# The squares for the MLP's norm, taken from the copy in DRAM during the first up groups

## The chip, the cores and the metric

One Trainium2 chip; the kernel runs on one of its cores. The metric is the time of one execution in device microseconds (us). The kernel before took 2325.93 us, the median of three runs (2322.78 to 2328.96).

A core has five engines that each work through their own instructions in order and wait for each other by semaphores: TensorE (PE, matrix products into the banks of PSUM), VectorE (DVE), ScalarE (ACT), GpSimd (POOL), and SyncE (SP), which here only issues transfers. SP's transfers go over eight lanes in turn (DMAHW0 to 7 in the orders below), POOL's over lanes named DMASW; a transfer waits for the one before it on its lane.

## The reference

One layer of an encoder block on 512 tokens of width 2048, in float32:

```
h   = rmsnorm(x, g_mix)                        # projection, two mixers side by side
x   = x + concat(mla, dsa) @ w_out             # 2048 x 2048
x   = x + cross_attention(rmsnorm(x, g_cross)) # ends in w_o_cross, 512 x 2048
hm  = rmsnorm(x, g_mlp)
x   = x + square(relu(hm @ w_up)) @ w_down     # 2048 x 8192 and 8192 x 2048
y   = rmsnorm(x, g_final)

rmsnorm(x, g) = x * rsqrt(mean(x * x, -1) + 1e-6) * g
```

The case is about the norm in front of the MLP. The kernel doesn't scale hm before the product: it multiplies the raw x with the gains into w_up and applies the squared factor 1/rms^2 to square(relu(...)) afterwards, so the factor is needed only when the first group of up is finished.

## The kernel before

All activations are kept transposed, features on the 128 partitions and the 512 tokens in the row. x is 16 tiles `res[0]` to `res[15]` of 128x512.

**Up.** 16 groups of 8 units. A unit is a Strassen-like step of 7 products with 6 matmuls of 128x256 each (42 matmuls, L308); the 8 units of a group add into the same 7 of 8 PSUM banks, products in the order p1, q6, p7, q4, p2, q5, p3. A unit needs its weights as a split: `load_blocks` issues three SP transfers into a ring of four buffers (L1461, L1463, L1465), POOL adds a further block by an accumulating transfer (L1470), and the split makes two sums on VectorE and, twice, a cast on ScalarE ("hi") and the rest on VectorE ("lo"), one part of 1024 and one of 768 columns. A ring buffer is free again when the split of the unit four before is done. A unit also needs the pair q of x (q is its number in the group, made once by `gen_xpair(q)`: gains on ScalarE, four sums, casts and lo parts).

**The end of a group** (`gen_up_out`, L1537): the 7 banks are emptied, the first (p1) by a ScalarE copy into e1, a part of the buffer G; then relu and square on ScalarE (four passes of 128x1024), the multiplication with `bc` (the squared 1/rms of each token, spread over the partitions) on VectorE, four sums, and two SP stores of 896 KB from G to `tp_dram` (L1596). G and its companion CT are there once: the next group's e1 goes into the part that these stores read.

**The squares.** `residual1(n)` (L1376) finishes a residual tile after the cross attention: it adds, spawns the pair of every second tile, stores the tile to `xs_dram` (L1385; down reads it again), squares it on ScalarE and adds the square to `acc_r` on POOL (L1393). When all 16 are in, `gen_rstd_l` (L1425) sums over the partitions by four ones-matmuls (L303, bank<-ones), takes the power -1/2 (VectorE, then POOL, `small<-small,nhalf`), spreads it by four transposes (L328) and a ScalarE copy into `bc`, and squares `bc` on VectorE.

The ring of the weights lies where residual tiles lay. So the loads of the first three units wait for the pairs that read those tiles, `("xg", q)`, and for the squares, `("sq", 1, 3)` and `("sq", 1, 7)` (L1449, L1451).

**What sets the order.** The kernel is written as generators that yield until something is ready. A planner (`Plan`, `Planned`) keeps a clock for each engine from fixed costs and lets the generators go on in the order of these clocks, which becomes the order of the instructions on each engine. It knows what TensorE, VectorE, ScalarE and POOL write and read, and of the transfers only what is told to it by `plan.issue("dma", ...)`; of the stores to `tp_dram` it is told nothing. The semaphores are placed afterwards for every true dependence, the reads of stores among them.

Of the kernel before, what the change touches and what calls it, by code (L numbers as in the profile page):

```python
# [11 lines left out]
AF = mybir.ActivationFunctionType  # L12
OP = mybir.AluOpType
# [4 lines left out]
KT = 16  # L18
# [140 lines left out]
def kernel(  # L159
# [20 lines left out]
    nc = tc.nc  # L180
# [3 lines left out]
    plan = Plan()  # L184
    act = Planned(nc.scalar, plan, "act")
    dve = Planned(nc.vector, plan, "dve")
    pool = Planned(nc.gpsimd, plan, "pool")
    rt = plan.ready
# [11 lines left out]
    xs_dram = nc.dram_tensor("xs_dram", (KT, 128, 512), F32, kind="Internal").ap()  # L200
# [12 lines left out]
    def fslot(i, n=512):  # L213
        return fb[:, i : i + n]
# [6 lines left out]
    res = [fslot(4096 + 512 * i) for i in range(8)] + [fslot(512 * i) for i in range(8)]  # L221
# [21 lines left out]
    flag = set()  # L243
# [16 lines left out]
    def step():  # L260
        for t in list(tasks):
            if not t.done and t.at <= plan.clk["pe"]:
                t.go()

    def spawn(gen, first=False):
        t = Task(gen)
        if first:
            tasks.insert(0, t)
        else:
            tasks.append(t)  # L270
        return t

    def until(cond):
        idle = 0
        while not cond():
            n = plan.count
            step()
            if plan.count == n and not cond():
                later = [t.at for t in tasks if t.at > plan.clk["pe"]]
                if later:  # L280
                    plan.clk["pe"] = min(later)
                else:
                    idle += 1
                    assert idle < 200, "schedule is stuck"
            else:
                idle = 0
# [89 lines left out]
    def rstd_tokens(dst, accs, ntb, n, home):  # L376

        yield rt(*accs)
        b = (yield from take(home))[0]
        for tb in range(ntb):  # L380
            for j, a in enumerate(accs):
                mm(b[:, 2 * tb : 2 * tb + 2], a[:, tb * 128 : tb * 128 + 128], ones,
                   j == 0, j == len(accs) - 1)
        yield rt(b)
        rsqrt_mean(dst, b[:, 0 : 2 * ntb : 2], n)
        home.put(b)
# [674 lines left out]
    acc_r, sq_r = s2[2], [s2[0], s2[1]]  # L1061
# [297 lines left out]
    sq_x = s2[4]  # L1359
# [16 lines left out]
    def residual1(n, b):  # L1376

        yield rt(b, res[n])
        dve.tensor_tensor(res[n], res[n], b, op=OP.add)
        banks_f.put(b)  # L1380
        flag.add(("x1", n))
        if n % 2:
            spawn(gen_xpair(n // 2), True)
        yield rt(res[n])
        nc.sync.dma_start(xs_dram[n], res[n])  # L1385
        while n > 0 and ("sq", 1, n - 1) not in flag:
            yield 0
        if n == 0:
            act.activation(acc_r, res[n], AF.Square)
        else:  # L1390
            act.activation(sq_x, res[n], AF.Square)
            yield rt(sq_x)
            pool.tensor_tensor(acc_r, acc_r, sq_x, op=OP.add)  # L1393
        flag.add(("sq", 1, n))

    def sums(dst, b12, b11, b21, b22, eng):
        t1, t2, t3, t4 = dst
# [5 lines left out]
    def gen_xpair(q):  # L1403

        while ("x1", 2 * q) not in flag or ("x1", 2 * q + 1) not in flag:
            yield 0
        gx = (yield from take(gxbufs))[0]
        x1, x2 = res[2 * q], res[2 * q + 1]
        g1, g2 = (g_mlp[:, 2 * q + j : 2 * q + j + 1] for j in range(2))
        yield rt(x1, x2)  # L1410
        act.activation(gx[:, 0:256], x1[:, 256:512], AF.Copy, scale=g1)
        act.activation(gx[:, 512:1024], x2, AF.Copy, scale=g2)
        act.activation(gx[:, 256:512], x1[:, 0:256], AF.Copy, scale=g1)
        yield rt(gx)
        c = lambda i: gx[:, 256 * i : 256 * i + 256]
        flag.add(("xg", q))
        sums([c(4), c(5), c(6), c(7)], c(0), c(1), c(2), c(3), dve)
        pr = yield from take_pair(q)
        for a, n in ((0, 768), (768, 1024)):
            src = gx[:, 256 + a : 256 + a + n]  # L1420
            yield from hi_lo(pr[:, a : a + n], pr[:, 1792 + a : 1792 + a + n], src)
        gxbufs.put(gx)
        XP[q] = pr

    def gen_rstd_l():  # L1425
        while ("sq", 1, 15) not in flag:
            yield 0
        yield from rstd_tokens(rstd_l, [acc_r], 4, D, banks_f)
        yield from spread(bc, rstd_l, 4)
        yield rt(bc)  # L1430
        dve.tensor_tensor(bc, bc, bc, op=OP.mult)
        flag.add("bc")

    def spread(dst, tok, ntb):

        yield rt(tok)
        b = (yield from take(banks_f))[0]
        for tb in range(ntb):
            transpose(blk(b, tb), tok[:, tb : tb + 1].to_broadcast([128, 128]))
        yield rt(b)  # L1440
        act.copy(dst, b[:, 0 : 128 * ntb])
        banks_f.put(b)


    def load_blocks(i):

        k = i - first_s
        if k == 0:
            need = lambda: all(("xg", q) in flag for q in range(2)) and ("sq", 1, 3) in flag  # L1449
        elif k < 3:  # L1450
            need = lambda: all(("xg", q) in flag for q in range(4)) and ("sq", 1, 7) in flag  # L1451
        elif k == 3:
            need = lambda: first_s - 2 in splits and splits[first_s - 2].done
        else:
            need = lambda: i - 4 in splits and splits[i - 4].done
        while not need():
            yield 0
        r, src = ring[k % 4], units[i].src
        s31 = r[:, 768:1280]
        a21 = src[:, 0:256].unsqueeze(1).to_broadcast([128, 2, 256])  # L1460
        nc.sync.dma_start(s31.rearrange("p (u c) -> p u c", u=2), a21)  # L1461
        plan.issue("dma", 800.0, [s31], [], 3800)
        nc.sync.dma_start(r[:, 0:512], src[:, 256:768])  # L1463
        plan.issue("dma", 800.0, [r[:, 0:512]], [], 3800)
        nc.sync.dma_start(r[:, 1536:1792], src[:, 768:1024])  # L1465
        plan.issue("dma", 400.0, [r[:, 1536:1792]], [], 3800)

        def add_blocks():
            yield rt(s31)
            nc.gpsimd.dma_start(s31, src[:, 256:768], accum_op=OP.add)  # L1470
            plan.issue("pool", 1250.0, [s31], [s31], 5000)
            flag.add(("load", i))

        spawn(add_blocks(), True)
# [29 lines left out]
    def strassen_pe(i, st, pair, first, last, order):  # L1504

        hi, lo = HI[units[i].buf], LO[units[i].buf]
        until(lambda: ("sa", i) in flag)
        for x, r in enumerate(order):
            w, t = PRODUCTS[r]
            if x == 4:  # L1510
                flag.add(("pa", i))
                until(lambda: ("sb", i) in flag)
            one_product(st, r, hi, lo, 256 * w, pair, t, first, last)
# [85 lines left out]
    def up_units(g):  # L1599
        st = {}  # L1600

        def pe(kk):
            def run(i):
                if g == 0 and kk == 0:
                    spawn(gen_rstd_l())
                until(lambda: kk in XP)
                if kk == 7:
                    spawn(gen_up_out(g, st), True)
                strassen_pe(i, st, XP[kk], kk == 0, kk == 7, ORDER)
                if g == 15:  # L1610
                    pace(2)
            return run

        return [Unit(w_up[g * 8 + kk], 1024, pe(kk)) for kk in range(8)]
# [11 lines left out]
    def pace(n):  # L1626
        for _ in range(n):
            if paced[0] < 4 * NLOAD:
                spawn(gen_load_t(*divmod(paced[0], 4)))
                paced[0] += 1  # L1630
# [350 lines left out]
    def loader():  # L1981
        for i, u in enumerate(units):
            if i >= first_s:
                yield from load_blocks(i)
                continue
            while i >= 3 and not (i - 3 in splits and splits[i - 3].done):
                yield 0
            more = u.load() if u.load is not None else iter(())
            for t in more:
                if t is True:  # L1990
                    break
                yield t
            if u.src is not None:
                dma(wraw[u.buf][:, 0 : u.n], u.src)
            yield from more
            flag.add(("load", i))
# [145 lines left out]
```

## Time and profile before

| | |
|---|---|
| median of 3 runs | 2325.93 us |
| profiled execution, its own time | 2329.6 us |
| its span (first to last instruction) | 2327.5 us |
| mean granted clock of TensorE | 0.991 of 2.4 GHz |
| TensorE busy | 2251.6 us, 97% |
| VectorE busy | 1662.7 us, 71% |
| ScalarE busy | 1067.2 us, 46% |
| POOL busy | 411.0 us, 18% |

The times of the rows are from the span's start. The residual tiles are made from about 911 to 949 us, up runs from 948 to about 1640. A busy share is a mean over stages; a stage is read from its own stretch. "Idle before" is the time an engine stood still before an instruction, with what released it.

### The profile page before, as it was taken

The numbers are of one execution on the slowest core, as the hardware profiler recorded it, in microseconds if no ns is written. First come the engines' busy times: TensorE is split into PE (matmuls) and PEld (weight loads), VectorE is DVE, ScalarE is ACT, GpSimd is POOL, SyncE is SP. The second block draws the span as 40 slices with busy tenths as digits, with TensorE's granted clock in tenths as the row PEclk, the third lists the DMA queues.
The fourth block names the chain that finished last, engine by engine and source line by source line (L and its number), as shares of the span: only waits on it lengthen the run. The fifth ranks groups of instructions, "written<-read, shape, count | busy, mean of one in ns | idle before, by whom it ended". The sixth has DMA issues, their size and how long they took to land.

```text
span 2327.5 us, 41732 instructions
## 1 busy us (share of the span) xinstructions
PE 2251.6 (97%) x16056; PEld 2165.0 (93%) x16056; DVE 1662.7 (71%) x2629; ACT 1067.2 (46%) x1506; POOL 411.0 (18%) x493
## 2 busy tenths in 40 slices
PE   8999999999999999899999999999999999999996
PEld 8999999998888787799999999999999999999996
DVE  7678543447834547978678787877977877877886
ACT  6542433345523446645354454545444444444453
POOL 3110010103001101411111111111112231111142
PEclk9999999999999999899999999999999999999998
DMA  5322222231243434687888978789889998778863
GB/s 174 103 89 89 68 82 75 71 109 46 82 150 113 144 132 155 169 211 202 226 223 215 251 209 248 205 231 277 245 237 245 231 230 233 219 215 232 220 172 107
DMA packets 272103, 403.56 MB, mean 173 GB/s; under 512 B 23552, under 2 KB 175120, under 8 KB 271648
## 3 DMA queue, kind: packets, MB, share of 16 engines
q1 hardware_dynamic: 229376, 328.41, 43.2%
q0 software_dynamic: 41296, 71.40, 18.2%
q8 instruction: 125, 2.05, 0.4%
q10 hardware_dynamic: 1232, 1.09, 0.2%
q14 instruction: 74, 0.61, 0.1%
HBM read 363.07 MB, written 37.75 MB: 172 GB/s over the span
## 4 chain that ended last, share of the span: by engine, by line
PE 65%; DVE 15%; DMA 11%; issue 5%; POOL 2%; ACT 1%; SPq 1%; DVEq 0%; POOLq 0%; ACTq 0%
PE bank L303 33%; PE bank L308 30%; DMA fb<-in_w_up_dram 7%; DVE fb L139 7%; DVE hl L139 6%; DMA fb<-in_w_dn_dram 2%; POOL fb L139 2%; PE bank L328 2%; DMA big<-tp_dram 2%; DVE big L139 1%; ACT hl L139 1%; SPq L1463 0%; SPq L1461 0%; ACT fb L139 0%; DMA tp_dram<-fb 0%
## 5 line engine op out<-in xcount | busy, mean ns | idle before, releaser
L308 PE MATMUL bank<-big,hl 128*128 128x256 f32 x10680 | 1304.2, 285 | 43.2 <-DVE hl L139 28.5
L308 PEld LDWEIGHTS bank<-big,hl 128*128 128x128 f32 x10680 | 1293.8, 193 | 53.2 <-DVE hl L139 35.9
L139 ACT CAST hl<-fb 128x1024 fp32r<-128x1024 f32 (+4 forms) x699 | 636.3, 924 | 925.2 <-PE bank L303 288.3
L139 DVE TENSOR_TENSOR hl<-fb,hl 128x768 fp32r<-128x768 f32 (+5 forms) x698 | 746.1, 1084 | 389.1 <-ACT hl L139 388.3
L303 PE MATMUL bank<-hl,big 128*128 128x384 f32 (+4 forms) x2916 | 524.5, 329 | 7.7 <-ACT big L139 6.7
L303 PEld LDWEIGHTS bank<-hl,big 128*128 128x128 f32 x2916 | 478.8, 189 | 18.7 <-ACT big L139 6.7
L139 DVE TENSOR_TENSOR fb<-fb 128x256 f32<-128x256 f32 (+3 forms) x763 | 387.8, 523 | 148.1 <-DMA fb<-in_w_up_dram 87.8
L303 PE MATMUL bank<-big,hl 128*128 128x512 f32 (+1 forms) x1192 | 296.1, 390 | 0.0
L139 POOL TENSOR_TENSOR fb<-fb 128x128 f32<-128x128 f32 (+5 forms) x203 | 158.5, 803 | 713.0 <-DVE fb L139 308.1
L303 PEld LDWEIGHTS bank<-big,hl 128*128 128x128 f32 x1192 | 222.2, 188 | 43.3
L1470 POOL DMA_DIRECT2D fb<-in_w_up_dram x128 | 110.6, 864 | 531.4 <-DVE hl L139 184.0
L1470 POOL DMA_DIRECT2D fb<-in_w_dn_dram x128 | 110.7, 865 | 497.2 <-DMA fb<-in_w_dn_dram 198.6
L139 DVE TENSOR_TENSOR fb<-fb,bank 128x512 f32<-128x512 f32 x226 | 149.4, 681 | 11.2 <-PE bank L308 2.2
L139 ACT ACTIVATE fb<-fb 128x512 f32<-128x512 f32 (+2 forms) x144 | 116.7, 814 | 77.7 <-DVE fb L139 56.5
L303 PE MATMUL bank<-big 128*128 128x256 f32 (+2 forms) x534 | 113.2, 327 | 2.0 <-DVE big L139 1.2
L303 PEld LDWEIGHTS bank<-big 128*128 128x128 f32 x534 | 87.1, 188 | 10.1 <-DVE big L139 2.5
L139 ACT CAST big<-bank 128x512 fp32r<-128x512 f32 (+2 forms) x119 | 61.2, 541 | 56.4 <-PE bank L328 28.4
L139 DVE TENSOR_TENSOR big<-bank,big 128x512 fp32r<-128x512 f32 (+1 forms) x102 | 62.7, 642 | 25.5 <-ACT big L139 25.4
L139 ACT CAST big<-big 128x1792 fp32r<-128x1792 f32 x32 | 54.2, 1694 | 49.9 <-DMA big<-tp_dram 45.6
L328 PE MATMUL bank<-cs,fb 128*128 128x128 f32 x384 | 60.2, 275 | 8.9 <-POOL fb L139 3.5
L139 DVE TENSOR_TENSOR big<-big 128x1792 fp32r<-128x1792 f32 x32 | 64.6, 2019 | 3.3 <-ACT big L139 3.3
L328 PEld LDWEIGHTS bank<-cs,fb 128*128 128x128 f32 x384 | 46.3, 140 | 17.2 <-POOL fb L139 5.8
(92 smaller groups left out, 765.2 us busy)
## 6 DMA issues: line engine op xcount, KB each, us to landing
fb<-in_w_up_dram SPq DMA_DIRECT2D x256, 256.0 KB, 5.0
fb<-in_w_dn_dram SPq DMA_DIRECT2D x256, 256.0 KB, 5.1
fb<-in_w_up_dram POOLq DMA_DIRECT2D x128, 256.0 KB, 5.9
fb<-in_w_dn_dram POOLq DMA_DIRECT2D x128, 256.0 KB, 5.8
fb<-in_w_in_dram SPq DMA_DIRECT2D x80, 384.0 KB, 3.0
tp_dram<-fb SPq DMA_DIRECT2D x32, 896.0 KB, 9.5
big<-tp_dram SPq DMA_DIRECT2D x128, 224.0 KB, 5.7
fb<-in_w_out_dram SPq DMA_DIRECT2D x32, 512.0 KB, 3.2
```

The source lines that it names most:

```text
L139: r = fn(*args, **kw)
L303: nc.tensor.matmul(out, lhsT, rhs, start=start, stop=stop)
L308: nc.tensor.matmul(out, lhsT, rhs, start=start, stop=stop, skip_group_check=True)
L328: nc.tensor.transpose(out, in_, ident)
L1470: nc.gpsimd.dma_start(s31, src[:, 256:768], accum_op=OP.add)
```

## The change

`residual1` no longer squares; it only marks the tile as stored. A new generator `gen_squares`, spawned with the first unit of up beside `gen_rstd_l`, reads the 16 tiles back from `xs_dram` (16 SP loads of 256 KB) into three buffers in turn, squares them on ScalarE and adds them on POOL. A buffer is loaded again when POOL has added it. Between two tiles it lets at least 1.8 us of the planner's TensorE clock pass. The loads of the first weights wait for the pairs alone.

```diff
@@ residual1 and the new generators
         yield rt(res[n])
         nc.sync.dma_start(xs_dram[n], res[n])
-        while n > 0 and ("sq", 1, n - 1) not in flag:
-            yield 0
-        if n == 0:
-            act.activation(acc_r, res[n], AF.Square)
-        else:
-            act.activation(sq_x, res[n], AF.Square)
-            yield rt(sq_x)
-            pool.tensor_tensor(acc_r, acc_r, sq_x, op=OP.add)
-        flag.add(("sq", 1, n))
+        flag.add(("st", n))
+
+    def gen_squares():
+
+        bufs = [sq_x, fslot(15360), fslot(15872)]
+        for n in range(KT):
+            b = bufs[n % 3]
+            while ("st", n) not in flag:
+                yield 0
+            if n < 3:
+                yield from load_sq(b, n)
+            yield rt(b)
+            act.activation(acc_r if n == 0 else b, b, AF.Square)
+            if n > 0:
+                yield rt(b)
+                pool.tensor_tensor(acc_r, acc_r, b, op=OP.add)
+            if n + 3 < KT:
+                spawn(load_sq(b, n + 3))
+            yield plan.clk["pe"] + 1800.0
+        flag.add(("sq", 1, 15))
+
+    def load_sq(b, n):
+        nc.sync.dma_start(b, xs_dram[n])
+        plan.issue("dma", 800.0, [b], [], 4000)
+        yield 0
@@ load_blocks
         if k == 0:
-            need = lambda: all(("xg", q) in flag for q in range(2)) and ("sq", 1, 3) in flag
+            need = lambda: all(("xg", q) in flag for q in range(2))
         elif k < 3:
-            need = lambda: all(("xg", q) in flag for q in range(4)) and ("sq", 1, 7) in flag
+            need = lambda: all(("xg", q) in flag for q in range(4))
@@ the first unit of up
                 if g == 0 and kk == 0:
                     spawn(gen_rstd_l())
+                    spawn(gen_squares())
```

The order of TensorE at the ones-matmuls, before. It is unit 1 of group 0; the rows are the products of that unit, six matmuls each, one bank for each product.

```order
L308 MATMUL bank_64<-big,hl 128x256 x3
L308 MATMUL bank_68<-big,hl 128x256 x6
L303 MATMUL bank_65<-ones,fb 128x2 [waits Pool_49]
L303 MATMUL bank_65<-ones,fb 128x2 x3
L308 MATMUL bank_63<-big,hl 128x256 x6
L308 MATMUL bank_66<-big,hl 128x256 x6
L308 MATMUL bank_70<-big,hl 128x256 [waits Activation_49]
```

And after the change, where they stand in unit 15, the last of group 1, up to the first two products of unit 16, which opens group 2.

```order
L308 MATMUL bank_68<-big,hl 128x256 x4
L303 MATMUL bank_69<-ones,fb 128x2 [waits Pool_49]
L303 MATMUL bank_69<-ones,fb 128x2 x3
L308 MATMUL bank_68<-big,hl 128x256 x2
L308 MATMUL bank_63<-big,hl 128x256 x6
L308 MATMUL bank_66<-big,hl 128x256 [waits Activation_49]
L308 MATMUL bank_66<-big,hl 128x256
L308 MATMUL bank_66<-big,hl 128x256 [waits DVE_49]
L308 MATMUL bank_66<-big,hl 128x256 x3
L308 MATMUL bank_70<-big,hl 128x256 x6
L328 MATMUL bank_69<-cs,small 128x128 [waits Pool_49]
L328 MATMUL bank_69<-cs,small 128x128 x3
```

```order
L308 MATMUL bank_67<-big,hl 128x256 x6
L308 MATMUL bank_69<-big,hl 128x256 [waits Activation_49]
L308 MATMUL bank_69<-big,hl 128x256 x5
L308 MATMUL bank_65<-big,hl 128x256 [waits Activation_49]
L308 MATMUL bank_65<-big,hl 128x256 x5
```

The ones-matmuls and the transposes behind them moved by 14 units; the transposes stand 20 matmuls behind the ones, and 12 matmuls later unit 16 wants bank_65.

The order of ScalarE at the end of group 1, before. COPY from bank_65 is the e1 of group 1; DMAHW0 and 1 in its waits are the two stores of group 0, whose passes stand far ahead of these rows.

```order
L139 CAST hl<-fb 128x768 [waits DVE_49,DMAHW7_49,PE_49,Activation_49]
L139 COPY fb<-bank_65 128x512 [waits DMAHW1_49,DMAHW0_49,PE_49]
L139 CAST hl<-fb 128x1024 [waits DMASW3_49,DMAHW2_49,DVE_49,DMAHW3_49,PE_49,Activation_49]
L139 COPY fb<-bank_70 128x512 [waits PE_49]
L139 CAST hl<-fb 128x768 [waits DVE_49,DMAHW4_49,PE_49,Activation_49]
```

And after: COPY from bank_69 makes `bc`, the four ACTIVATE are relu and square of group 0, and the copy from bank_65 is again e1 of group 1, with the two stores of group 0 as DMAHW7 and 0.

```order
L139 COPY fb<-bank_69 128x512 [waits DVE_49,PE_49]
L139 CAST hl<-fb 128x768 [waits DMAHW0_49,PE_49,Activation_49]
L139 ACTIVATE fb<-fb 128x1024
L139 ACTIVATE fb<-fb 128x2x2x256 [waits Activation_49]
L139 ACTIVATE fb<-fb 128x1024
L139 ACTIVATE fb<-fb 128x2x2x256 [waits Activation_49]
L139 COPY fb<-bank_65 128x512 [waits DMAHW7_49,DMAHW0_49,DVE_49]
L139 COPY fb<-bank_70 128x512 [waits DVE_49]
```

The passes of group 0 now stand right ahead of the first copy of group 1.

The order of SP in groups 0 and 1 after the change; L1477, L1479 and L1481 are the weight loads of a unit (L1461, L1463, L1465 before), L1408 the loads of the squares, which before did not stand between them.

```order
L1477 DMA fb<-in_w_up_dram 128x2x256 [waits DMAHW3_49,DMASW1_49,DVE_49]
L1479 DMA fb<-in_w_up_dram 128x512 [waits DMAHW4_49]
L1481 DMA fb<-in_w_up_dram 128x256 [waits DMAHW5_49]
L1408 DMA fb<-xs_dram 128x512 [waits DMAHW6_49,Pool_49]
L1408 DMA fb<-xs_dram 128x512 [waits DMAHW7_49,Pool_49]
L1477 DMA fb<-in_w_up_dram 128x2x256 [waits DMAHW0_49,DMASW2_49,DVE_49]
```

One or two loads of squares, each with a wait for POOL, moved in ahead of the weight loads of a unit.

## Rows read from the trace of the kernel before

**Rows 1.** TensorE's timeline: start, us, instructions, idle before and releaser.

```profile
951.49 3.14 PE L308 MATMUL bank<-big,hl 128*128 128x256 f32 x24 [2.40 <-DVE hl L139]
955.70 2.17 PE L308 MATMUL bank<-big,hl 128*128 128x256 f32 x16 [1.07 <-DVE hl L139]
960.58 0.50 PE L308 MATMUL bank<-big,hl 128*128 128x256 f32 x2 [2.71 <-ACT hl L139]
964.72 2.50 PE L308 MATMUL bank<-big,hl 128*128 128x256 f32 x10 [3.65 <-DVE hl L139]
967.02 1.70 PE L303 MATMUL bank<-ones,fb 128*128 128x2 f32 x8
968.59 3.55 PE L308 MATMUL bank<-big,hl 128*128 128x256 f32 x15
971.93 1.05 PE L328 MATMUL bank<-cs,small 128*128 128x128 f32 x4
972.64 115.69 PE L308 MATMUL bank<-big,hl 128*128 128x256 f32 x951
...
1174.75 364.90 PE L308 MATMUL bank<-big,hl 128*128 128x256 f32 x3024 [1.46 <-DVE fb L139]
```

**Rows 2.** Stretches: us; PE, PEld, DVE, ACT, POOL busy (instructions); clock, DMA, GB/s.

```profile
951.00:965.00 14.00, 6.09 (x43) 5.48 (x44) 13.90 (x17) 10.13 (x17) 7.56 (x6) 0.86 0.76 196
966.00:968.00 2.00, 2.00 (x12) 2.00 (x11) 0.60 (x1) 0.00 (x0) 0.00 (x0) 0.50 0.00 0
980.40:1046.20 65.80, 65.80 (x550) 65.80 (x549) 50.79 (x73) 33.03 (x39) 11.21 (x13) 1.00 0.82 210
```

**Rows 3.** POOL by form, 911 to 965: count, busy us, mean ns, idle before.

```profile
L139 POOL TENSOR_TENSOR fb<-fb 128x512 f32<-128x512 f32 x15 | 23.4, 1563 | 106.9 <-ACT fb L139 104.4 <-DMA fb<-in_w_up_dram 2.4
```

**Rows 4.** VectorE by form, 911 to 965, the seam.

```profile
L139 DVE TENSOR_TENSOR fb<-fb 128x256 f32<-128x256 f32 x27 | 14.9, 585 | 0.4
L139 DVE TENSOR_TENSOR hl<-fb,hl 128x1024 fp32r<-128x1024 f32 x7 | 12.5, 1780 | 5.0 <-ACT hl L139 5.0
...
L139 DVE TENSOR_TENSOR big<-fb,big 128x768 fp32r<-128x768 f32 x5 | 7.4, 1487 | 0.0
L139 DVE TENSOR_TENSOR big<-fb,big 128x1024 fp32r<-128x1024 f32 x5 | 7.3, 1466 | 0.0
```

**Rows 5.** VectorE by form, 980.4 to 1046.2, thirteen units without adds.

```profile
L139 DVE TENSOR_TENSOR hl<-fb,hl 128x1024 fp32r<-128x1024 f32 x13 | 15.9, 1221 | 6.4 <-ACT hl L139 6.4
L139 DVE TENSOR_TENSOR fb<-fb 128x256 f32<-128x256 f32 x30 | 12.4, 422 | 6.1 <-DMA fb<-in_w_up_dram 5.5
L139 DVE TENSOR_TENSOR hl<-fb,hl 128x768 fp32r<-128x768 f32 x13 | 12.3, 952 | 2.2 <-ACT hl L139 2.2
L139 DVE TENSOR_TENSOR fb<-fb 128x512 f32<-128x512 f32 x6 | 3.9, 685 | 0.0
```

**Rows 6.** SP's timeline: the two stores of group 0.

```profile
1024.97 1.30 SPq L1596 DMA_DIRECT2D tp_dram<-fb x2
```

**Rows 7.** ScalarE's timeline: passes of group 0, and the e1 copy of group 1.

```profile
1005.61 1.06 ACT L139 ACTIVATE fb<-fb 128x1024 f32<-128x1024 f32 x1
1006.57 1.04 ACT L139 CAST hl<-fb 128x1024 fp32r<-128x1024 f32 x1
...
1041.05 0.83 ACT L139 CAST hl<-fb 128x768 fp32r<-128x768 f32 x1 [1.11 <-DMA fb<-in_w_up_dram]
1041.85 0.59 ACT L139 COPY fb<-bank 128x512 f32<-128x512 f32 x1
```

**Rows 8.** The stores' line, all 32: from issue to landing.

```profile
DMA to landing us min/median/max: 6.7/9.5/11.6
```

**Rows 9.** POOL's timeline: the power.

```profile
969.00 1.15 POOL L139 TENSOR_TENSOR small<-small,nhalf 128x4 f32<-128x4 f32 x1 [5.43 <-DVE small L139]
```

**Rows 10.** The page: POOL's accumulating transfers, and the weight loads (KB each, us to landing).

```profile
L1470 POOL DMA_DIRECT2D fb<-in_w_up_dram x128 | 110.6, 864 | 531.4 <-DVE hl L139 184.0
...
fb<-in_w_up_dram SPq DMA_DIRECT2D x256, 256.0 KB, 5.0
```

## The prediction

> **What bounds the kernel now.** I read the busy times first: TensorE works 97% of the span, so only its idle time and its slow clock are to be had or lost. TensorE's timeline then shows where these are near the change [rows 1]. At the seam where the cross-attention output ends and the up groups begin it stands still four times, 2.40, 1.07, 2.71 and 3.65 us, together 9.83 us, always for the casts and the "lo" parts that VectorE and ScalarE make of the new weights and of the new pairs. Behind the seam it hardly stops: in group 3 to 11, 3024 matmuls in 364.90 us, 0.1207 us each, is its full rate. A unit of up (42 matmuls) is thus 5.07 us.
>
> Why it stands still, the busy times by stretch tell [rows 2]: from 951 to 965 VectorE works 13.90 of 14.00 us and TensorE 6.09. VectorE bounds the seam. Its own operations are longer there than elsewhere. Beside the 15 adds of POOL [rows 3] a 128x1024 lo takes 1780 ns and a 128x256 sum 585 ns [rows 4]; in the quiet stretch from 980 they take 1221 and 422 ns [rows 5].
>
> **What the change removes at the seam.** The 15 adds leave it, and with them the stretching. With the quiet lengths VectorE would save 27 x 0.163 = 4.4, 7 x 0.559 = 3.9, 5 x (1.487 - 0.952) = 2.7 and 5 x (1.466 - 1.221) = 1.2 us, 12.2 us in all [rows 4, 5]. Most is saved while TensorE still has work of the projection, and shows only as a better start of the pairs. It does not remove the bound: for a unit and its pair VectorE needs two sums, a 1024 lo and a 768 lo for the weights (2 x 0.42 + 1.22 + 0.95 = 3.0) and four sums and two lo parts for the pair (4 x 0.42 + 1.22 + 0.95 = 3.85), 6.85 us against 5.07 of TensorE. Three pairs (q 5 to 7) are still to be made when units are being multiplied, 3 x 1.8 = 5.3 us.
>
> The standing time is not all the loss. From the last gap on the clock is at half (granted 0.50, which is 1.2 GHz [rows 2]): the 10 + 15 matmuls from 964.72 and 968.59 take 6.05 us where 3.02 is the full rate, and the 951 from 972.64 take 0.9 us over it [rows 1]. That is 3.9 us for the clock. So the seam can give at most 9.8 + 3.9 = 13.7 us. With 5.3 left I take **-8.4 us**, bounds 0 and -13.7. That the weights of units 0 to 2 no longer wait for the squares serves the same gain.
>
> **What it moves: the ones-matmuls.** The sum of squares ends in four ones-matmuls (x8 records), POOL's power, and four transposes. They stood in unit 1 of group 0; they now stand in unit 15, the last of group 1, since the planner lets 1.8 us of its TensorE clock and more pass between squares. Everything of group 0 that needs "bc" comes after that: four ScalarE passes, two multiplications, four sums and the two stores to tp_dram. But the first evacuation of group 1 writes e1 into the part of G from which those stores read. In the order of ScalarE that copy (out of bank_65) waits for the lanes 7 and 0 of the DMA, which are the two stores; it stands ahead of all other evacuations of group 1. And TensorE's second product of unit 16 goes into the same bank_65. Before, the stores were issued at 1024.97 [rows 6] and the copy came at 1041.85 [rows 7], 16.9 us later, with the landing at most 11.6 us after issue [rows 8]: some 5 us of slack. Now the order is turned around.
>
> Let T0 be the start of the ones-matmuls. TensorE wants bank_65 at T0 + 5.2: 0.85 for the ones (half of 1.70, which is at half clock), 20 matmuls x 0.1207 = 2.4, 0.5 for the transposes (half of 1.05), 12 more matmuls 1.45 [rows 1]. The copy takes the long way:
> - T0 + 3.8: transposes done; POOL's power (1.15 [rows 9]) is done before their turn.
> - ScalarE copies bc (0.59), casts 768 (0.83), then four passes at a pitch of 0.96, 1.06 long [rows 7]: T0 + 9.3.
> - VectorE multiplies after the last one (1.22, as a 1024 lo) and makes four sums of 0.685 [rows 5]: T0 + 13.3.
> - SP issues two stores at 0.65 each [rows 6]; the second is issued at T0 + 14.0 and lands 9.5 later, 6.7 to 11.6 [rows 8]: T0 + 23.5.
> - The copy, 0.59: T0 + 24.1.
>
> TensorE is held 24.1 - 5.2 = **+18.9 us**, with the spread of the landing 16.1 to 21.0. ScalarE waits in the copy for most of it, and the casts for unit 18 on stand behind it; those of unit 17 are ahead of it, so TensorE has two units of work, 10 us, when it is released, and ScalarE needs some 6 us for what is queued until the next cast pair. I cost that at nothing; without that cover it would be the 1 to 2 us of a late cast.
>
> **Clock after the hold.** Four stops of together 9.8 us cost 3.9 at the seam; the stop of 1.46 us before 1174.75 is followed by matmuls at full rate [rows 1]. One stop of 19 us lies nearer to the first: **+3**, bounds 0 and 3.9.
>
> **The moved squares themselves.** VectorE has 65.80 - 50.79 = 15.0 us to spare in thirteen units from 980 [rows 2], and the 15 adds now spread over sixteen units. Stretching as at the seam costs it 12.2 us: it fits, **0**, and if that cover were gone it would be a few us. On that point the Trainium skill ("SBUF — State Buffer", section "SBUF: two separate sides") speaks against the change: an operation of GpSimd and one of VectorE with two SBUF inputs exclude each other on a shared port, and the loser waits the whole instruction out. By this rule the term would be the fifth rival's 3 in place of 0. The trace bears it out in part: VectorE's operations are stretched by 12.2 us beside 23.4 us of adds [rows 3, 4, 5], not blocked for all of it.
>
> Squares are loaded again, 16 loads of 256 KB on SP's queue, each (from the fourth) waiting for POOL's add of three squares before, with weight loads queued behind it, and POOL's accumulate (0.864) behind the weights' landing (5.0 us [rows 10]). Per two units that is a ring: 5.0 + 0.9 + 2 x 1.56 (the adds) + 0.8 for issue, 9.8 us, against 10.1 that TensorE needs. It just fits; I take **+1**, bounds 0 and 6 (one landing and an accumulate late). The 16 ScalarE squares of 128x512 are no more than before and lie in ScalarE's idle half (33.03 of 65.80 busy [rows 2]). The small stops from 1089 to 1174 (four, the last of 1.46 us [rows 1]) may go or stay: 0, bound -4.
>
> **Sum.** -8.4 + 18.9 + 3 + 0 + 1 = +14.5 on the profiled execution's 2329.6 us: 2344.1. That execution lies 3.7 us above the median of 2325.93; against the median it is **2340**.
>
> **Rivals.** About 0.3%, 7.0 us, is what a measurement can tell from no change here (2319 to 2333).
> - No hold, the other side: the copy finds the stores landed, or the transposes come so early that the chain ends before the bank is wanted. It decides at T0 + 5.2; the stores alone take at least 6.7 us. The gain of the seam is then all there is: 2325.9 - 8.4 to 13.7, about 2312 to 2318. For it: before had 5 us of slack at this place. Against: the order of ScalarE. 8 in 100.
> - The whole seam gain, 13.7, and a short hold, 16.1, with no clock loss: +2.4, about 2328 to 2330. For it: VectorE loses its only disturbance. Against: 6.85 us over 5.07. 15 in 100.
> - The change doesn't empty the seam: VectorE is bound by the pairs alone, gain 0: 18.9 + 3 + 1 = +23, 2349. 8 in 100.
> - The ring of loads, accumulates and adds falls behind, and the ones-matmuls wait too: +6 in place of +1, 2345 to 2350. For it: 9.8 against 10.1. 10 in 100.
> - Every add holds VectorE up for its whole length: 15 x 1.563 = 23.4 us, against 15.0 to spare and the 5.2 (2 x 1.22 + 4 x 0.685) of group 0's end that move out of the stretch. VectorE falls 3 us behind: 2343. For it: a 256 sum takes 0.16 more beside the adds. Against: no operation at the seam is longer by an add's length on the mean. 7 in 100. (It is the page's rule above, carried out.)
>
> **Chances.** The forecast has 52. Its own range is 2330 to 2350. The range for eight in ten takes in the second rival below and the third above: 2325 to 2351. Slower by over 0.3%: most of the forecast, the third to fifth rival, 0.73. Within: the second rival and the low edge of the forecast, 0.18. Faster: 0.09.
>
> **What would show it.** After: no ones-matmul in group 0, and VectorE's 1024 lo at 1.22 us and its sums at 0.42 before 965; 4 to 6 us of standing time at the seam in place of 9.8; a single stop of TensorE of 16 to 21 us at the start of group 2, released by ScalarE's copy, which itself waits for tp_dram; half clock for a few us after it. I am wrong if that stop is under 10 us, if the seam gives nothing, or if stops of over 1 us are strewn over groups 0 and 1 with loads of weights as their cause.

## The result, and the profile after

The changed kernel is slower: 2345.0 us in its first four runs, a ratio of 1.0080 to the kernel before (95% interval 1.0065 to 1.0094); in six more runs, beside the last experiments, 2341.7 us and 1.0070 (1.0052 to 1.0089). The forecast was 2340, range 2325 to 2351. The profiled execution took 2339.93 us, span 2338.2.

TensorE's timeline after, the rows that answer to [rows 1] (start, us, instructions, idle before and releaser):

```profile
949.61 20.55 PE L308 MATMUL bank<-big,hl 128*128 128x256 f32 x170
972.42 4.63 PE L308 MATMUL bank<-big,hl 128*128 128x256 f32 x24 [2.25 <-DVE hl L139]
977.55 20.42 PE L308 MATMUL bank<-big,hl 128*128 128x256 f32 x168 [0.50 <-DVE hl L139]
998.64 5.42 PE L308 MATMUL bank<-big,hl 128*128 128x256 f32 x42 [0.67 <-DVE hl L139]
1004.83 29.29 PE L308 MATMUL bank<-big,hl 128*128 128x256 f32 x242 [0.78 <-DVE hl L139]
1035.93 1.05 PE L303 MATMUL bank<-ones,fb 128*128 128x2 f32 x8 [1.81 <-POOL fb L139]
1036.84 4.04 PE L308 MATMUL bank<-big,hl 128*128 128x256 f32 x20
1040.68 0.75 PE L328 MATMUL bank<-cs,small 128*128 128x128 f32 x4
1041.19 1.90 PE L308 MATMUL bank<-big,hl 128*128 128x256 f32 x12
1059.17 41.04 PE L308 MATMUL bank<-big,hl 128*128 128x256 f32 x319 [16.09 <-ACT fb L139]
```

Four stops at the seam (9.83 us) have become one of 2.25 us, with 1.95 us in three small ones behind it, and no ones-matmuls stand in group 0. Where they stand now, TensorE waits 1.81 us for POOL's last add; and in place of the seam's stops there is one of 16.09 us at the start of group 2, which ScalarE releases. How it comes about is read from ScalarE's timeline, [rows 7] before:

```profile
1041.47 0.59 ACT L139 COPY fb<-bank 128x512 f32<-128x512 f32 x1 [2.24 <-PE bank L328]
1042.10 0.84 ACT L139 CAST hl<-fb 128x768 fp32r<-128x768 f32 x1
1042.85 4.18 ACT L139 ACTIVATE fb<-fb 128x1024 f32<-128x1024 f32 x4
1058.53 1.07 ACT L139 COPY fb<-bank 128x512 f32<-128x512 f32 x2 [11.51 <-DMA tp_dram<-fb]
```

The first row makes bc, the third is group 0's four passes, and the last, group 1's e1 copy, has waited 11.51 us for a transfer that the profile names: the store to tp_dram. SP's timeline has that store, [rows 6] before, and the stores' own time to landing was this, [rows 8] before:

```profile
1050.97 1.30 SPq L1612 DMA_DIRECT2D tp_dram<-fb  x2
```

```profile
DMA to landing us min/median/max: 4.9/5.9/6.8
```

VectorE by form at the seam, 911 to 965, is back at its quiet lengths ([rows 4] had 585 and 1780 ns):

```profile
L139 DVE TENSOR_TENSOR fb<-fb 128x256 f32<-128x256 f32 x38 | 14.8, 422 | 0.6
L139 DVE TENSOR_TENSOR hl<-fb,hl 128x1024 fp32r<-128x1024 f32 x9 | 11.0, 1221 | 6.3 <-ACT hl L139 6.3
```

But the stretching has moved with the adds. The same forms from 972 to 1036, in groups 0 and 1:

```profile
L139 DVE TENSOR_TENSOR hl<-fb,hl 128x1024 fp32r<-128x1024 f32 x13 | 20.2, 1555 | 3.0 <-ACT hl L139 2.9
L139 DVE TENSOR_TENSOR fb<-fb 128x256 f32<-128x256 f32 x23 | 19.5, 848 | 4.4 <-DMA fb<-in_w_up_dram 4.0
L139 DVE TENSOR_TENSOR hl<-fb,hl 128x768 fp32r<-128x768 f32 x12 | 12.9, 1071 | 0.8 <-ACT hl L139 0.7
```

And POOL's adds in the same groups:

```profile
L139 POOL TENSOR_TENSOR fb<-fb 128x512 f32<-128x512 f32 x15 | 25.7, 1714 | 10.0 <-ACT fb L139 8.2 <-DMA fb<-in_w_up_dram 1.6
```

Against [rows 5] that is 13 x 0.334 + 23 x 0.426 + 12 x 0.119 = 15.6 us, beside 25.7 us of adds. Most of it fits into VectorE's spare time; what doesn't shows in the 1.95 us of small stops. POOL's adds are stretched as well: 1714 ns, where the two adds of the kernel with transfers below take 1276.

### The profile page after: what moved, and what is told of

It reads as the page before. It is cut to its first block, busy times and chain, and to the rows that moved or that the text cites. A ratio compares the mean times of both kernels' runs of the same rounds, so it can differ in the third digit from the quotient of the medians.

```text
span 2338.2 us, 41779 instructions
## 1 busy us (share of the span) xinstructions
PE 2253.2 (96%) x16056; PEld 2166.5 (93%) x16056; DVE 1666.6 (71%) x2629; ACT 1070.6 (46%) x1506; POOL 411.6 (18%) x493
## 4 chain that ended last, share of the span: by engine, by line
PE 70%; DVE 11%; DMA 9%; issue 4%; POOL 2%; ACT 2%; SPq 1%; DVEq 0%; POOLq 0%; ACTq 0%
PE bank L308 35%; PE bank L303 33%; DVE fb L139 5%; DVE hl L139 5%; DMA fb<-in_w_up_dram 5%; POOL fb L139 2%; DMA fb<-in_w_dn_dram 2%; PE bank L328 2%; DMA big<-tp_dram 2%; DVE big L139 1%; ACT hl L139 1%; ACT fb L139 1%; DMA fb<-xs_dram 1%; SPq L1479 0%; ACT big L139 0%
## 5 line engine op out<-in xcount | busy, mean ns | idle before, releaser
L139 ACT CAST hl<-fb 128x768 fp32r<-128x768 f32 (+4 forms) x699 | 639.6, 927 | 928.9 <-PE bank L303 291.0
L139 DVE TENSOR_TENSOR fb<-fb 128x256 f32<-128x256 f32 (+3 forms) x763 | 393.9, 531 | 143.0 <-DMA fb<-in_w_up_dram 85.7
L139 DVE TENSOR_TENSOR big<-bank,big 128x512 fp32r<-128x512 f32 (+1 forms) x102 | 62.9, 643 | 25.7 <-ACT big L139 25.6
```

The costliest lines, as they stand in the source:

```text
L139: r = fn(*args, **kw)
```

## The experiments

A stretch of up says more than a whole time, since executions of one kernel differ by some us (2318 to 2336 in the runs of before). The table has, beside the ratio of times, the us from the first matmul of up to its 646th (in the changed kernel the last ahead of the ones-matmuls) and to its 1694th (about 40 units), both from TensorE's timeline of the one profiled execution, adding up the counts; a few missing records make these good to about 1 us. A single profiled execution also differs from the next one of the same kernel: the two of the changed kernel lie 3.0 us apart to matmul 646.

| kernel | ratio (95%) | to 646 | to 1694 | late stop (start of group 2) |
|---|---|---|---|---|
| before | 1 | 94.1 | 226.3 | none |
| after | 1.0080 (1.0065-1.0094) | 84.5 | 237.7 | 16.09 |
| after, once more | 1.0070 (1.0052-1.0089) | 87.5 | 238.2 | 16.45 |
| late bc in the kernel before | 1.0079 (1.0055-1.0104) | 92.6 | 240.6 | 15.78 |
| own tiles for group 1 | 1.0033 (1.0018-1.0048) | 87.4 | 234.1 | 4.46, 2.39 |
| no time between squares | 1.0044 (1.0023-1.0064) | 89.6 | 237.1 | 16.17 |
| both of these | 1.0002 (0.9990-1.0015) | 88.2 | 226.7 | 9.89 (unit 18) |
| adds of 4 columns | 1.0040 (1.0026-1.0054) | 81.4 | 232.2 | 16.45 |
| before without adds | 0.9932 (0.9906-0.9957) | 82.7 | 209.1 | none |
| 8 to 15 in place, 0 to 7 read back | 0.9995 (0.9983-1.0006) | 98.2 | 224.3 | none |
| the same, 1.2 us between | 1.0027 (1.0014-1.0041) | 91.5 | 229.5 | 10.62 |
| half and half | 0.9988 (0.9975-1.0001) | 93.4 | 223.6 | none |
| half and half, later, own tiles | 1.0001 (0.9988-1.0014) | 91.8 | 221.1 | none |
| adds as transfers | 0.9949 (0.9929-0.9968) | 86.4 | 213.9 | none |

One part of the change needed no run: with the two `("sq", ...)` conditions of `load_blocks` taken out of the kernel before, the order of instructions on all five engines stays the same, row by row. (The true waits on the squares stay in that kernel, since ScalarE there reads the tiles that the weights replace.)

**Late bc in the kernel before.**

```diff
-        while ("sq", 1, 15) not in flag:
+        while ("sq", 1, 15) not in flag or "late" not in flag:
...
+                if g == 1 and kk == 7:
+                    flag.add("late")
```

> The kernel before, squares and adds where they were, but the ones-matmuls held back to the start of unit 15 (matmul 632 of up; in the changed kernel it is 646). One part of the change alone. Theory: the same hold without any gain at the seam: a stop of 13 to 16 us at the start of group 2, 2 to 3 us of half clock after it, seam stops still 9.8 us in sum: about 2325.6 + 17 = 2343, 2339 to 2347. Rival (the slowdown comes from the loads of the squares and POOL's adds in groups 0 and 1): no stop over 5 us, 2324 to 2329.

Measured 2347.0 us, the upper end of what the theory gave. The seam's stops are those of before, and the hold is there without any reload:

```profile
965.77 22.95 PE L308 MATMUL bank<-big,hl 128*128 128x256 f32 x168 [3.17 <-DVE hl L139]
...
1062.67 84.08 PE L308 MATMUL bank<-big,hl 128*128 128x256 f32 x678 [15.78 <-ACT fb L139]
```

So the late bc alone costs as much as the whole change. The rival, loads and adds in groups 0 and 1, has fallen as the main cause.

**Own tiles for group 1's temporaries.**

```diff
+        if g == 1:
+            e1, e5, u2, u3 = (fslot(o) for o in (9472, 10496, 15360, 15872))
+            while ("scaled", 0) not in flag:
+                yield 0
...
```

> The changed kernel, but group 1 of up puts its four temporaries (e1, e5, u2, u3) into four free tiles, so its first evacuation copy no longer has to wait for group 0's two stores; bc comes as late as in the changed kernel. Theory (the hold is the copy behind the stores): TensorE's stop at the start of group 2 shrinks from 16.1 us to what the four late ScalarE passes of group 0 leave, 4 to 6 us, and the time falls by about 11 us from the changed kernel's 2345 to 2334. Rival (the hold is bc and ScalarE's passes, the stores are only named last): the stop stays at 14 us or more, 2343 to 2346. Rival (the loss lies elsewhere, in loads behind POOL's adds): the stop may go but the time stays within 3 us of 2345.

Measured 2335.0. The stop shrank to 4.46 and 2.39 us:

```profile
1052.96 1.65 PE L308 MATMUL bank<-big,hl 128*128 128x256 f32 x6 [4.46 <-ACT fb L139]
1057.01 43.06 PE L308 MATMUL bank<-big,hl 128*128 128x256 f32 x336 [2.39 <-DVE fb L139]
```

So 9.2 of the 16.1 us were the wait for the stores, and bc's own lateness is what is left: the copy stands behind group 0's four passes, and VectorE's part of the evacuation behind group 0's sums. Between matmul 646 and 1694 the profiles differ by 6.5 us (153.2 and 146.7).

**No time between the squares.**

```diff
-            yield plan.clk["pe"] + 1800.0
+            yield plan.clk["pe"] + 0.0
```

> The changed kernel with 0 in place of the 1800 ns between two squares. In the order the ones-matmuls move from matmul 646 of up to 537, 109 matmuls or 13.2 us earlier. Theory (the hold is as long as bc is late): the stop at the start of group 2 shrinks from 16.1 us by what is gained, to 2 to 6 us, while TensorE waits longer than 1.8 us for POOL's adds ahead of the ones-matmuls (3 to 8 us): 2330 to 2338. Rival (a length that doesn't depend on bc's time): the stop stays above 12 us, 2343 to 2348.

Measured 2339.4, and a miss for the theory: bc came 13 us earlier, and the stop did not shrink, as the rival has it; the time lies between the two. TensorE's, SP's and ScalarE's timelines, and the stores' time to landing:

```profile
1022.90 1.05 PE L303 MATMUL bank<-ones,fb 128*128 128x2 f32 x8 [1.29 <-POOL fb L139]
...
1059.04 84.19 PE L308 MATMUL bank<-big,hl 128*128 128x256 f32 x678 [16.17 <-ACT fb L139]
```

```profile
1045.34 0.38 SPq L1477 DMA_DIRECT2D fb<-in_w_up_dram  x1
...
1046.77 1.88 SPq L1612 DMA_DIRECT2D tp_dram<-fb  x2
```

```profile
1058.40 1.08 ACT L139 COPY fb<-bank 128x512 f32<-128x512 f32 x2 [15.50 <-DMA tp_dram<-fb]
```

```profile
DMA to landing us min/median/max: 7.8/9.4/10.9
```

The planner laid group 0's passes between the casts of later weights, and the last sum ended at 1042.5, 19.6 us after the ones-matmuls began; in the changed kernel this took 15.0. The stores then stand behind the weight loads that wait for VectorE to free a buffer (the loads at 1045.34) and were issued after 23.9 us, where the changed kernel, with no loads in the way, again needs 15.0. And with these loads just ahead of them they took longer to land, so that the copy began after 35.5 us and not after 22.6. Of the 13 us won, about 4.6 thus went into the passes, 4.3 into SP's order and 4.1 into the landing. The length of the hold is not a function of bc's time alone.

**Both edits.** The two edits above together.

> The two edits together that alone did not remove the hold: no time between squares (ones-matmuls at matmul 537 in the order) and group 1's temporaries in free tiles, so that its first copy doesn't wait for the stores of group 0. With the first alone the stop stayed at 16.17 us, since the stores stood late in SP's order (issued at 1046.77, behind weight loads) however early bc came; with the second alone 4.46 and 2.39 us were left, for bc was late. Theory (both are needed: bc ahead of the group's end and no wait for the stores): no stop over 3 us at the start of group 2; what is left is the seam's gain, less the waits in groups 0 and 1: 2318 to 2326. Rival (bc alone decides and the stores are only named last): a stop of 10 us or more stays, 2332 to 2340.

Measured 2327.5: too slow for the theory, too fast for the rival. The copy no longer waits; but the wait has moved on. ScalarE's timeline, and TensorE's:

```profile
1058.56 1.06 ACT L139 ACTIVATE fb<-fb 128x1024 f32<-128x1024 f32 x1 [13.66 <-DMA tp_dram<-fb]
```

```profile
1060.60 0.80 PE L308 MATMUL bank<-big,hl 128*128 128x256 f32 x2 [9.89 <-ACT hl L139]
```

Now it is group 1's square pass, which writes into G, that waits for the stores; the casts of unit 18, at whose start TensorE stops, stand behind it. Group 0's sums had ended at 1043.2, but the stores were issued only at 1049.84, again behind weight loads (1048.43). The stores hold whatever comes first on ScalarE and writes where they read.

**Adds of 4 columns.**

```diff
-                pool.tensor_tensor(acc_r, acc_r, b, op=OP.add)
+                pool.tensor_tensor(acc_r[:, 0:4], acc_r[:, 0:4], b[:, 0:4], op=OP.add)
```

> The changed kernel with POOL's 15 adds cut to 4 of 512 columns (the sum of squares is complete for 4 tokens only); the place of the ones-matmuls in the order is the same, matmul 646. It measures what the adds themselves cost in groups 0 and 1. Theory: the stop at the start of group 2 stays at 16 us within 1; the wait for POOL ahead of the ones-matmuls (1.81 us, with 1.6 us of half clock behind it) goes, and the stops of 2.25, 0.50, 0.67 and 0.78 us shrink to half: 3 to 6 us less than the changed kernel, 2339 to 2342. Rival (the adds fit into what VectorE and POOL have to spare, as the prediction's 0 has it): within 2 us of 2345. Rival (they stretch VectorE at the group's end and so lengthen the hold): the stop shrinks to under 14 us.

Measured 2334.6, less than the theory's 2339 to 2342. The hold stays, 16.45 us; VectorE's 256 sums are at 423 ns, the stretch to matmul 646 is 3 to 6 us shorter, and to 1694 5.5 to 6. By the times it is 7 to 9 us. The adds thus cost about 6 us in groups 0 and 1, where the prediction took 0 for VectorE and 1 for POOL.

**The kernel before without the adds.**

```diff
-            yield rt(sq_x)
-            pool.tensor_tensor(acc_r, acc_r, sq_x, op=OP.add)
```

> The kernel before without POOL's 15 adds of the squares (the sum of squares is left out: bc then comes from the first tile alone); everything else, ScalarE's squares too, stays in place. Theory (the seam stops come from VectorE's operations being stretched beside the adds): VectorE's 1024 lo at the seam takes 1.22 us and its 256 sum 0.42, the seam stops fall from 9.8 us to 2 to 5, half clock less, and the time falls by 7 to 11 us to about 2317. Rival (VectorE is bound by the pairs anyway): seam stops 8 us or more, 2323 to 2327. Rival (the gain is from ScalarE's squares or from weight loads that no longer wait): the same, no gain here.

Measured 2314.1. One stop of 2.81 us is left at the seam, and none for the next 1991 matmuls:

```profile
958.90 0.58 PE L308 MATMUL bank<-big,hl 128*128 128x256 f32 x1 [2.81 <-DVE hl L139]
...
959.98 240.22 PE L308 MATMUL bank<-big,hl 128*128 128x256 f32 x1991
```

So the adds are what the seam's stops come from. Leaving them out is worth 0.4 to 0.9%, 13.2 us by the medians where 7 to 11 were expected: the later stops of before went too.

**Tiles 8 to 15 in place.** They lie untouched until the end of group 0, so only 0 to 7 are read back.

```diff
...
+        for j, n in enumerate([*range(8, KT), *range(8)]):
+            b = res[n] if n >= 8 else bufs[n % 3]
             yield rt(b)
...
+            act.activation(b if j else acc_r, b, AF.Square)
...
-            yield plan.clk["pe"] + 1800.0
```

> The changed kernel, with bc earlier: tiles 8 to 15, which lie untouched until the end of group 0, are squared in place without a reload from the start of up, and only tiles 0 to 7 are read back. In the order the ones-matmuls then stand in unit 9 (matmul 380) and not in unit 15. Theory: the stores of group 0 are issued before group 1's first copy needs them, the stop at the start of group 2 is gone, and what is left is the seam's gain, less some stretching of VectorE in units 0 to 8 (0 to 5 us): 2316 to 2322. Rival (adds right after the seam slow VectorE as they did before it): seam stops back to 8 us or more in units 0 to 8, 2324 to 2328. Rival (bc is not the cause): the stop of 16 us stays, 2345.

Measured 2327.5, in the rival's range. No hold, as the theory has it, but the gain went into new waits around nine adds in a row on POOL: the stop of 4.17 us falls beside them, while VectorE needs 4.23 us for two lo parts, and that of 6.30 comes after the accumulating transfer of a unit's weights that stood behind them. POOL's timeline, and TensorE's:

```profile
972.22 16.50 POOL L139 TENSOR_TENSOR fb<-fb 128x512 f32<-128x512 f32 x9
988.66 0.87 POOL L1489 DMA_DIRECT2D fb<-in_w_up_dram  x1
```

```profile
978.33 18.73 PE L308 MATMUL bank<-big,hl 128*128 128x256 f32 x142 [4.17 <-DVE hl L139]
1003.36 0.80 PE L308 MATMUL bank<-big,hl 128*128 128x256 f32 x2 [6.30 <-ACT hl L139]
```

**The same with 1.2 us between the squares.**

> The version with tiles 8 to 15 squared in place and 0 to 7 read back, now with 1.2 us of the planner's clock between two squares, so that at most five adds stand in a row on POOL in place of nine, most often one or two between accumulating transfers; the ones-matmuls move from matmul 380 to 499, unit 11. Theory: the stops of 4.17, 6.30 and 2.41 us that came from accumulating transfers behind nine adds shrink to 5 us in sum, and bc still comes early enough: a stop of 0 to 3 us at the start of group 2; 2316 to 2322. Rival (VectorE has no room for the stretching in units 4 to 8 however the adds are spaced): 2323 to 2328 with stops of over 8 us in sum in these units.

Measured 2334.0: stops of 4.24 and 3.05 us stay in units 4 to 9, with two small ones 8.65 us where it was 14.11, and the stores (issued at 1045.12) hold TensorE 10.62 us. Both theories missed the hold.

**Half and half.** Tiles 0 to 7 as before; 8 to 15 squared in place, added during group 0.

> A new division: tiles 0 to 7 are squared and added as each residual tile is made, as before; tiles 8 to 15 are squared in place where they lie and added during group 0, with 1.8 us of the planner's clock between two; nothing is read back. The ones-matmuls then stand at matmul 252 of up, in unit 6. Theory: half the adds left the seam and no hold appears: seam stops 3 to 6 us in place of 9.8, no stop over 3 us later, 2316 to 2322. Rival (the first eight adds are enough to keep VectorE behind): seam stops 8 us or more, 2323 to 2328. Rival (eight adds between the accumulating transfers of units 4 to 8 hold up weights, as in the version with nine of them in a row): single stops of 3 us and more in units 4 to 8, 2322 to 2328.

Measured 2325.8, where the first rival had it. No hold, but 6.60 us in one stop at the seam and 9.73 in three: the first eight adds and those of units 0 to 4 still fall beside the making of the pairs. That these are the cause is argued here, and tested in part by the next version. With the second eight only when the pairs are done, and own tiles for group 1:

> The version with tiles 0 to 7 added as before and 8 to 15 squared in place, whose adds now begin only when all eight pairs of x are made, and with group 1's temporaries in free tiles. Theory (adds beside the making of the pairs are what stretches the seam): the seam stop of 6.60 us falls to 2 to 4 us, no hold: 2316 to 2322. Rival (four adds in a row on POOL hold up the accumulating transfers of units 5 to 9, as in the version with nine): stops of over 5 us in sum there, 2322 to 2328.

Measured 2325.7, no difference from before. The seam stop is 4.98 us, more than the theory's 2 to 4, so the second eight adds were a small part of it. The stretch to 1694 is 5 us shorter than in before, but the whole time doesn't show it.

**Adds as transfers.**

```diff
...
-            pool.tensor_tensor(acc_r, acc_r, sq_x, op=OP.add)
...
+            nc.gpsimd.dma_start(a, b, accum_op=OP.add)
...
```

> The kernel before with 13 of POOL's 15 adds replaced by accumulating transfers from tile to tile (three sums side by side, two adds at the end); tiles 0 to 7 as they are made, 8 to 15 squared in place; nothing is read back, and the ones-matmuls stand at matmul 247. Theory (it is POOL's tensor operations that stretch VectorE at the seam, not the squares or the traffic): VectorE's 1024 lo at the seam takes 1.22 to 1.3 us, the seam stops fall to 2 to 5 us and nothing is held later: 2312 to 2320. Rival (256 KB more traffic for each tile on the queues that bring the weights): weights land later, stops of 5 us and more on loads in units 0 to 6, 2323 to 2332.

Measured 2313.3. Its sum of squares is not the right one (why is open), so this is a probe and not a version to use. VectorE's 1024 lo at the seam takes 1219 ns beside it:

```profile
L139 DVE TENSOR_TENSOR hl<-fb,hl 128x1024 fp32r<-128x1024 f32 x8 | 9.7, 1219 | 6.0 <-ACT hl L139 6.0
```

And POOL's two adds that are left, at the end:

```profile
L139 POOL TENSOR_TENSOR fb<-fb 128x512 f32<-128x512 f32 x2 | 2.6, 1276 | 3.1 <-DMA fb<-fb 3.0
```

The transfers of 256 KB that POOL issues leave VectorE's lengths alone here, where POOL's tensor operations don't.

**The changed kernel once more.**

> The changed kernel once more, beside the others: its first four runs gave a ratio of 1.008 (2345.0), while its profiled execution lies 10.3 us over that of before and its first 40 units of up take 11.7 us more. Theory: the rows' difference is the whole change and the rest scatter between executions: ratio 1.004 to 1.007, 2336 to 2342. Rival (something costs time that the profiled execution doesn't show): 1.007 to 1.010, 2343 to 2350.

Measured 1.0070, on the border between the two. The rows show 11.4 and 11.9 us in the first 40 units; the medians 15 to 19 us. The rest isn't explained by any row that was read. Part of it may be which execution was profiled: in the first set that of the changed kernel is the fastest of its four, that of before 3.7 us above its median.

## Why the prediction was right, point by point

- **The bound.** VectorE beside POOL's adds at the seam: right, shown by the kernel without the adds and by the one with transfers.
- **Seam, -8.4.** Right in kind, a little small. Of the 13.7 us at the seam a stop of 2.25 us and 1.7 us of slow clock behind it are left (24 matmuls in 4.63 us where 2.90 is full rate), 4.0 us where 5.3 were expected. To matmul 646 the two profiles of the changed kernel gain 9.6 and 6.6 us; in before this stretch still has the ones-matmuls and transposes, 1.35 us at full rate, and in the changed kernel it has the stops of 1.95 us beside the moved adds. That weights which no longer wait for the squares serve the gain is not shown: the loosened conditions of `load_blocks` change nothing by themselves, and with squares and conditions in place but no adds the first loads of units 1 to 3 are already issued at 936 to 940 us, where before has 943 to 946 and the changed kernel 930 to 938.
- **The hold, +18.9.** 16.09 and 16.45. From T0 = 1035.93 the chain came as listed: passes done at 1047.0 (T0 + 11.1, expected 9.3), sums done and stores issued from 1050.97 (T0 + 15.0, expected 13.3), the copy starts at 1058.53. The stores landed in 4.9 to 6.8 us and not in the 9.5 of [rows 8], and TensorE wanted the bank at 1043.09, T0 + 7.2 and not 5.2, since the 20 matmuls took 4.04 us where 2.41 is full rate (granted clock 0.50 from 1038 to 1040). The mechanism is shown by two kernels: late bc alone brings the hold, own tiles take most of it away.
- **Clock after the hold, +3.** 319 matmuls took 41.04 us where 38.5 is full rate: 2.5.
- **VectorE and POOL in groups 0 and 1, 0 and +1.** Too small: about 6 us by the kernel with thin adds. VectorE's stretching was 15.6 us, more than the 12.2 taken over from the seam, and the ones-matmuls waited 1.81 us for POOL (1.06 in the second profile). The Trainium skill ("SBUF — State Buffer", section "SBUF: two separate sides") has such operations shut each other out for a whole instruction. The rows are nearer to it than the prediction allowed. VectorE's 15.6 us stand beside 25.7 us of adds, but these adds are themselves longer than elsewhere: at 1276 ns the 15 would take 19.1 us. So neither this comparison nor the prediction's, 12.2 us beside 23.4 at the seam, where an add took 1563 ns, shows that the operations are not shut out in full; that stays open.
- **Later stops, 0.** 1.68 and 1.32 us in place of 1.25, 0.43, 1.52 and 1.46.
- **The sum.** +14.5 against 10.3 us between the two profiled executions and 15 to 19 by the medians. The two errors of size, a hold 3 us too long and adds some 5 us too cheap, went against each other: that the sum comes out so near is in part luck.
- **Slips.** The 3024 matmuls that give the full rate are those of groups 5 to 13, not 3 to 11, since 1692 matmuls stand ahead of them; the rate is the same. And T0 + 9.3 adds up to 9.2.
- **What was not seen.** The prediction treats the hold as fixed to T0. Bringing bc forward by 13 us (no time between squares) left it as it was. How the planner spreads the passes, the stores' place in SP's order behind weight loads that wait for VectorE, and a landing that is longer beside such loads belonged in the chain from the start.

## What to carry to other kernels

Work that is moved off a crowded stretch is paid for where its last consumer sits: follow the result (here bc) to the first instruction that writes where something behind it still reads, transfers included, which a planner may not know of. Moving that result forward by 13 us did not help here, since what lies between it and the landing of the stores grew by as much; look at when the store is issued and lands, not at when its data could be ready. And an operation that slows a neighbour engine does so at its new place too; it is cheaper only where that neighbour has time to spare and nothing urgent stands behind it in the queue.

## What the runs showed of the hardware that was not expected

A 128x256 sum on VectorE took 848 ns beside POOL's adds in groups 0 and 1 and 422 without them, the 768 lo only 1071 against 952. The two 896 KB stores of group 0 landed in 4.9 to 6.8 us in the changed kernel, where SP issued no weight load between 1045.40 and 1068.46, against 8.2 to 11.2 before, with weight loads right ahead of them and behind. And the accumulating transfers from tile to tile, 13 of them at 966 ns of POOL each, eight of these between 911 and 965, left VectorE's 1024 lo there at 1219 ns and its 256 sums at 420.
